# Fourteen pairs of the first feed-forward's up projection by seven products, with all sums of weight blocks made in memory

## The chip, the cores and the metric

The kernel runs on one core of one Trainium2 chip. A core has a matrix engine (TensorE, PE), a vector engine (VectorE, DVE), a scalar engine (ScalarE, ACT), a general engine (GpSimd, POOL) and SyncE (SP), which issues transfers. ACT and POOL can issue transfers too. The metric is device time in microseconds (us) from one launch, lower is better; it is given as the median of several runs, and beside it stands one execution taken by the hardware profiler.

## The reference

What is computed is a trunk of two decoder layers over 512 tokens of 1024 features, in fp32. Cut to what matters:

```python
for i in range(2):
    h = rms_norm(x, pre_g[i])
    h = even_mixer(h, ...) if i == 0 else odd_mixer(h, ...)
    x = x + rms_norm(h, post_g[i])
    h = conv_ffn(rms_norm(x, ffn_pre_g[i]), ffn_w_up[i], ffn_conv_w[i], ffn_conv_b[i], ffn_w_down[i])
    x = x + rms_norm(h, ffn_post_g[i])

def conv_ffn(h, w_up, conv_w, conv_b, w_down):       # w_up: 1024 x 5632, w_down: 2816 x 1024
    u = causal_dwconv(h @ w_up, conv_w, conv_b)      # three taps along the tokens, per feature
    gate, up = split(u, 2)
    return (silu(gate) * up) @ w_down
```

The first mixer runs latent attention (8 heads) and differential attention (4 heads) side by side and projects their joined heads. The second does the same with dilated-window attention (12 heads in three groups) and stick-breaking attention (4 heads).

## The kernel before

**Products.** Every fp32 weight and activation is split into two parts, a rounded one (h) and the rest (l), and a product is three matmuls (`mm3`, L343: h by h, h by l, l by h). The class `Weights` (L43) is the stream of weight tiles: SP loads a tile `wraw` (three buffers), ACT rounds it into `wh` (L81), DVE subtracts to get `wl` (L82), a few tiles ahead of use.

**The two feed-forwards** (`ffn`, L428). The up projection goes over 22 pairs of a gate block and an up block, 128 features each, over 512 tokens. A plain pair is 2 x 8 products of 512 columns (48 matmuls). A pair "by seven products" is the scheme of Strassen and Winograd over a 2 x 2 split: the weight tile of a pair has four blocks (half of the input features by gate or up), the activations have four (half of the features by half of the tokens), and seven block products, of 4 x 3 matmuls of 256 columns each, take the place of eight (84 matmuls). It needs sums of weight blocks and sums of activation blocks (`x_sums`, L488, once for a feed-forward), and puts the results together in PSUM. One half of the results comes out negated for some taps, which `minus` (L435) turns in the convolution's weights.

`SEVEN` (L37) says which pairs go so. In the first feed-forward these are 4, 6, ..., 18, every second one, eight in all. Their weight sums are made on the spot: `up_sums` (L175) loads the pair's two tiles, makes four block sums with DVE (L191, L192, L195, L198) and splits the result, and `seven_sums` (L568) runs the products. In the second feed-forward these are 4 to 17, fourteen in one row, in an order written out by hand (`begin_seven`, `seven`, L610 to L664: the scaling and convolution of one pair stand between the products of the next). Their block sums come ready from memory, as tiles of 128 x 512 next to the plain blocks (`up_blocks`, L204).

**The sums in memory.** `make_sums` (L145) writes them with transfers on POOL's queue. A chunk is three pairs, 384 rows of 512 numbers; four tensors `ws` hold four kinds of sums. A chunk takes eight moves in a chain: plain ones copy a block into `ws`, adding ones add a block to what lies there.

```python
steps = [(0, 3, ALU.bypass), (2, 2, ALU.bypass), (0, 2, ALU.add), (2, 0, ALU.add), (1, None, ALU.bypass),
         (1, 0, ALU.add), (3, -1, ALU.bypass), (3, 1, ALU.add)]
```

Fourteen pairs are five chunks, the last of two pairs. Two chunks (`EARLY`, L40) are moved in the first mixer, after the latent attention's shared norms (call at L1133); three in the second, after its first value products (L1550). A mark goes ahead: a transfer of one number into each first target, from a tile that is written at the place where the moves are to begin, so that they don't start earlier. The order runs chunks against each other with a lag of four steps.

**POOL's other work.** POOL takes its instructions in order. It computes every inverse root of a mean square (`rstd`, L256: L260, L262, L263). In the differential attention it does so for each of 16 units (L1321, L1322): `value` sums squares on ACT, POOL adds epsilon and raises to the power -1/2, and one iteration later `norm` (L1329) multiplies with it on DVE. That stage's loop (L1404) runs in an order written by hand on PE, DVE, ACT and POOL; PE's gaps are filled with projections (`fill`). At the end of the first feed-forward four rows of 128 tokens are normed twice, transposed (L293) and go into the second mixer's value products, in a written order as well. The second mixer's output rows use `rstd` again (L1856, L1862).

Outside the written orders a planner places the instructions of an engine.

Of the kernel before, what the change touches and what calls it, by code (L numbers as in the profile page):

```python
# [9 lines left out]
F32 = mybir.dt.float32  # L10
# [26 lines left out]
SEVEN = range(4, 19, 2), range(4, 18)  # L37
CHUNK = 3
PAIRS = len(SEVEN[1])
EARLY = 2  # L40
# [55 lines left out]
def trunk(tc, A, out):  # L96
# [3 lines left out]
    with ExitStack() as top:  # L100
# [44 lines left out]
        def make_sums(chunks, mark):  # L145

            wide = "(a q) c -> a (q c)"
            if not sums_of:
                sums_of[1] = [[dpool.tile([CHUNK * P, S], F32, tag=f"ws{j}{c}", name="ws")
                               for c in range(-(-PAIRS // CHUNK))] for j in range(4)]  # L150
            tiles = sums_of[1]

            def move(c, j, src, op=ALU.bypass):
                n = min(CHUNK, PAIRS - c * CHUNK) * P
                if src is None:
                    src = tiles[0][c][:n]
                elif src < 0:
                    src = tiles[1][c][:n]
                else:
                    src = A["ffn_up_q"][src, c * CHUNK * P:c * CHUNK * P + n]  # L160
                nc.gpsimd.dma_start(tiles[j][c][:n].rearrange(wide, q=4), src.rearrange(wide, q=4), accum_op=op,
                                    max_dma_last_dim=2048)

            steps = [(0, 3, ALU.bypass), (2, 2, ALU.bypass), (0, 2, ALU.add), (2, 0, ALU.add), (1, None, ALU.bypass),
                     (1, 0, ALU.add), (3, -1, ALU.bypass), (3, 1, ALU.add)]
            with tc.manual_schedule(engines={POOL.engine}):
                for c in chunks:
                    for j in (0, 2):
                        nc.gpsimd.dma_start(tiles[j][c][0:1, 0:1], mark)
                for n in range(len(steps) + 4 * len(chunks)):  # L170
                    for j, c in enumerate(chunks):
                        if 0 <= n - 4 * j < len(steps):
                            move(c, *steps[n - 4 * j])

        def up_sums(src):  # L175


            raws = []
            lo, hi = slice(0, S), slice(S, 2 * S)

            def unit(n):
                if n == 0:
                    for z in range(2):
                        raws.append(wpool.tile([P, 1024], F32, tag="wraw", name="wraw", bufs=3))
                        nc.sync.dma_start(raws[z][:], src[z])
                a, b = raws
                h, l = W.pair()
                if n == 0:
                    W.split(h, l, a, 1024)
                elif n == 1:  # L190
                    DVE.tensor_tensor(a[:, lo], a[:, lo], b[:, lo], ALU.add)  # L191
                    DVE.tensor_tensor(b[:, lo], b[:, lo], b[:, hi], ALU.add)  # L192
                    W.split(h, l, b, 1024)
                elif n == 2:
                    DVE.tensor_tensor(b[:, hi], b[:, hi], a[:, lo], ALU.add)  # L195
                    W.split(h, l, b[:, hi], S)
                else:
                    DVE.tensor_tensor(a[:, hi], a[:, hi], b[:, hi], ALU.add)  # L198
                    W.split(h, l, a, 1024)
                return h, l  # L200

            return [lambda n=n: unit(n) for n in range(4)]

        def up_blocks():  # L204

            def block(i, j):
                if j < 4:
                    return A["ffn_up_q"][j, i * P:(i + 1) * P]
                return sums_of[1][j - 4][i // CHUNK][i % CHUNK * P:(i % CHUNK + 1) * P]

            parts = [lambda i=i, j=j: block(i, j)
                     for i, j in ([(0, 0)] + [(i + (j == 0), j) for i in range(PAIRS)
                                              for j in (4, 1, 5, 0, 6, 7, 3)]) if i < PAIRS]
            return [(tuple(parts[n:n + 2]), S * len(parts[n:n + 2])) for n in range(0, len(parts), 2)]

        def ffn_units(layer):
            up = []
            for f in range(NF):
                if f in SEVEN[0] and layer == 0:
                    up += up_sums(A["ffn_w_up"][layer, f])  # L220
                elif f == SEVEN[1][0] and layer:
                    up += up_blocks()
                elif layer == 0 or f not in SEVEN[1]:
                    up += [(A["ffn_w_up"][layer, f, z], 1024) for z in range(2)]
            return (up + [lambda n=n: down[layer](n) for n in range(4 * HF)])
# [202 lines left out]
        def ffn(layer, xnT, pending, final):  # L428
            with ExitStack() as es:
# [138 lines left out]
                def seven_sums(u, p5):  # L568

                    z1, z2 = u[0][:, :256], u[0][:, 256:]  # L570
                    c21, c22 = u[1][:, :256], u[1][:, 256:]
                    def product(o, w, half, x, fresh):
                        for k in range(4):
                            b = slice(half * S + k * P, half * S + (k + 1) * P)
                            xs = [v[:, k] if isinstance(x, list) else v[:, k * 256:(k + 1) * 256] for v in x]
                            mm3(o, w[0][:, b], w[1][:, b], *xs, fresh and k == 0, k == 3, not fresh)

                    wa = W.next()
                    product(c21, wa, 0, x_block(0, 0), True)
                    ACT.copy(z1, c21)  # L580
                    wb = W.next()
                    p = bank("t", "p5")[:, :256]
                    product(p, wb, 0, sums[0], True)
                    ACT.copy(p5, p)
                    wc = W.next()
                    product(c21, wc, 0, sums[1], False)
                    DVE.tensor_tensor(z2, c21, p5, ALU.add)  # L587
                    product(z1, wa, 1, x_block(4, 0), False)
                    wd = W.next()
                    product(c21, wd, 0, sums[2], False)  # L590
                    DVE.tensor_tensor(c22, c21, p5, ALU.add)
                    product(z2, wd, 1, x_block(4, 256), False)
                    product(c21, wb, 1, sums[3], False)

# [84 lines left out]
                for n, f in enumerate(PAIRED):  # L679
# [6 lines left out]
                    if final and n == pairs[0]:  # L686
                        depth, W.depth = W.depth, 0
                        ready, stop = W.pos + 3, W.pos + (7 * PAIRS + 1) // 2 + 2
                        W.ahead(ready)
                        written = tc.manual_schedule(engines={PE.engine, DVE.engine, ACT.engine})  # L690
                        written.__enter__()
                        begin_seven()
                    if final and n in pairs:
                        left = seven(n, left)
                        if n == pairs[-1]:
                            for step in late:
                                step()
# [4 lines left out]
                    u = u4[2 * n:2 * n + 2] if n < 2 else [bank(t, "u") for t in "sa"] if n in pairs else [None] * 2  # L702
                    y = sp.tile([P, 2, S], F32, tag="y", name="y")
                    if n in pairs:
                        seven_sums(u, y[:, 1, :256])
                    scale, conv, silu, rest = left = evict(n, y, u)
                    for z in range(2):
# [6 lines left out]
                        if z == 0 or not final or n != pairs[0] - 1:  # L714
                            scale(z)
                        if not final or n != pairs[0] - 1:
                            conv(z)
                    if not final or n != pairs[0] - 1:
                        silu()
                        for step in rest:  # L720
                            step()
# [199 lines left out]
        def even():  # L921
            with ExitStack() as es:
# [51 lines left out]
                with ExitStack() as e1:  # L974
# [116 lines left out]
                    with ExitStack() as e2:  # L1091
# [41 lines left out]
                        make_sums(range(EARLY), rk[0:1, 0:1])  # L1133
# [265 lines left out]
                units = [(h, i) for h in range(4) for i in ORDER]  # L1399
                scored, turned_, valued = {}, {}, {}  # L1400
                plan = ((6, 2),) + ((2, 2),) * 11 + ((2, 1),) * 4 + ((1, 0), (1, 1), (1, 2), (0, 2))
                depth, W.depth = W.depth, 0
                with tc.manual_schedule(engines={PE.engine, DVE.engine, ACT.engine, POOL.engine}):
                    for n in range(len(units) + 4):  # L1404
# [13 lines left out]
                        if n >= 2 and n - 2 < len(units):  # L1418
                            valued[n - 2] = value(*units[n - 2])(turned_.pop(n - 2))
                        fill(plan[n][1])  # L1420
# [43 lines left out]
        def odd(xnT, pending, order):  # L1464
            xh, xl = xnT
            with ExitStack() as es:
# [414 lines left out]
def layout(inputs):  # L1881
# [50 lines left out]

    q = r["ffn_w_up"][1, SEVEN[1][0]:SEVEN[1][-1] + 1].reshape(PAIRS, 2, P, 2, S)
    r["ffn_up_q"] = q.transpose(1, 3, 0, 2, 4).reshape(4, PAIRS * P, S)
# [47 lines left out]
```

## Time and profile before

| | |
|---|---|
| median of 3 runs | 1134.77 us (1133.51 to 1138.42) |
| profiled execution, first to last instruction | 1130.8 us |
| PE busy | 1118.5 us, 6432 matmuls |
| DVE busy | 898.1 us |
| ACT busy | 624.9 us |
| POOL busy | 96.0 us |
| moved by DMA | 166.82 MB, 29.36 MB of them on POOL's queue |

The profiled execution has no time of its own beside its span; the median lies 4.0 us above the span, which is what surrounds the first and last instruction. A row of a timeline has the start in us, the duration in us, the engine, the line of the kernel, the operation, output and inputs with their shapes, a count if several are merged, and in brackets how long the engine stood before it and what released it. "PEld" are weight loads, "POOLq" and the like are an engine's sequencer. A DMA row on POOL is the issue of the transfer, not the transfer.

### The profile page before, as it was taken

How to read it: one execution, taken by the hardware profiler on the slowest of the kernel's cores; microseconds unless marked ns; L12 is line 12 of the kernel's file. 1: busy time of each engine (PE TensorE's matmuls, PEld its weight loads, DVE VectorE, ACT ScalarE, POOL GpSimd, SP SyncE). 2: the span in 40 equal slices, each digit the busy share in tenths (PEclk: the TensorE clock that was granted, in tenths of full speed). 3: DMA queues.
4: the chain of work that ended last, by engine and by line, in shares of the span. 5: the costliest groups of instructions: out<-in, count | busy, mean ns of one | idle time of the engine just before them, and what ended most of it. 6: DMA issues, size and time to landing. Idle time of an engine off the chain costs nothing.

```text
span 1130.8 us, 17165 instructions
## 1 busy us (share of the span) xinstructions
PE 1118.5 (99%) x6432; PEld 951.1 (84%) x6432; DVE 898.1 (79%) x1526; ACT 624.9 (55%) x1060; POOL 96.0 (8%) x189
## 2 busy tenths in 40 slices
PE   9999999999999999999999999999999999999997
PEld 8876677898998998887888877888999999988886
DVE  6677476489998898898984476576889999989887
ACT  5565466446555555556653455575456666645662
POOL 2211012220000000000031111102000000000002
PEclk9999999999999999999999999999999999999999
DMA  8666731131422333354737878852335556524461
GB/s 296 197 180 137 215 109 57 57 134 57 130 94 79 128 94 121 99 168 151 226 128 227 206 186 202 217 122 85 110 112 182 179 182 196 177 89 148 144 205 75
DMA packets 61426, 166.82 MB, mean 148 GB/s; under 512 B 7841, under 2 KB 8993, under 8 KB 61217
## 3 DMA queue, kind: packets, MB, share of 16 engines
q1 hardware_dynamic: 47712, 132.65, 36.2%
q0 software_dynamic: 11712, 29.36, 11.8%
q10 hardware_dynamic: 1920, 3.74, 1.0%
q8 instruction: 50, 0.82, 0.3%
q14 instruction: 32, 0.25, 0.1%
HBM read 158.35 MB, written 35.68 MB: 172 GB/s over the span
## 4 chain that ended last, share of the span: by engine, by line
PE 88%; DVE 5%; DMA 3%; issue 2%; ACT 1%; POOL 0%; SPq 0%; POOLq 0%; DVEq 0%; ACTq 0%
PE u L345 12%; PE u L347 12%; PE u L346 12%; PE acc L345 4%; PE acc L346 4%; PE acc L347 4%; PE apt L345 3%; PE apt L346 3%; PE apt L347 2%; PE ao L345 2%; PE ao L347 2%; PE ao L346 2%; DVE wl L82 2%; PE sps L1170 2%; DMA wraw<-in_ffn_w_down 1%
## 5 line engine op out<-in xcount | busy, mean ns | idle before, releaser
L81 ACT CAST wh<-wraw 128x1024 fp32r<-128x1024 f32 (+1 forms) x235 | 240.7, 1033 | 158.0 <-PE u L346 51.6
L82 DVE TENSOR_TENSOR wl<-wraw,wh 128x1024 fp32r<-128x1024 f32 (+1 forms) x235 | 280.6, 1201 | 52.5 <-ACT wh L81 51.9
L345 PE MATMUL u<-xh,wh 128*128 128x256 f32 (+1 forms) x680 | 223.5, 329 | 0.0
L346 PE MATMUL u<-xl,wh 128*128 128x256 f32 (+1 forms) x680 | 223.1, 328 | 0.0
L347 PE MATMUL u<-xh,wl 128*128 128x256 f32 (+1 forms) x680 | 222.9, 328 | 0.0
L345 PEld LDWEIGHTS u<-xh,wh 128*128 128x128 f32 x680 | 129.2, 190 | 12.6 <-DVE u L587 1.3
L347 PEld LDWEIGHTS u<-xh,wl 128*128 128x128 f32 x680 | 129.1, 190 | 11.2 <-DVE wl L82 0.3
L346 PEld LDWEIGHTS u<-xl,wh 128*128 128x128 f32 x680 | 129.3, 190 | 11.0
L345 PE MATMUL acc<-wh,gh 128*128 128x512 f32 (+1 forms) x250 | 96.9, 388 | 0.8 <-DVE uu L758 0.8
L346 PE MATMUL acc<-wl,gh 128*128 128x512 f32 (+1 forms) x250 | 96.9, 388 | 0.0
L347 PE MATMUL acc<-wh,gl 128*128 128x512 f32 (+1 forms) x250 | 96.9, 387 | 0.0
L522 ACT ACTIVATE y<-u,cw 128x512 f32<-128x512 f32 x88 | 67.6, 777 | 36.9 <-PE u L347 33.4
L345 PE MATMUL u<-gh,wh 128*128 128x256 f32 x264 | 74.9, 284 | 0.1
L260 POOL TENSOR_TENSOR rv<-ms,epst 128x1 f32<-128x1 f32 x39 | 12.3, 314 | 736.3 <-ACT junk L312 351.2
L347 PE MATMUL u<-gh,wl 128*128 128x256 f32 x264 | 74.7, 283 | 0.0
L346 PE MATMUL u<-gl,wh 128*128 128x256 f32 x264 | 74.7, 283 | 0.0
L526 DVE SCALAR_TENSOR_TENSOR y<-u,cw,y 128x511 f32<-128x511 f32 x88 | 65.0, 743 | 3.5 <-ACT y L522 3.4
L528 DVE SCALAR_TENSOR_TENSOR y<-u,cw,y 128x510 f32<-128x510 f32 x88 | 65.3, 745 | 1.5
L345 PEld LDWEIGHTS acc<-wh,gh 128*128 128x128 f32 x250 | 46.9, 188 | 11.2 <-DVE uu L758 1.4
L347 PEld LDWEIGHTS acc<-wh,gl 128*128 128x128 f32 x250 | 47.0, 188 | 9.7
L346 PEld LDWEIGHTS acc<-wl,gh 128*128 128x128 f32 x250 | 47.0, 188 | 9.4
L345 PEld LDWEIGHTS u<-gh,wh 128*128 128x128 f32 x264 | 50.6, 192 | 1.3 <-ACT u L580 0.5
(371 smaller groups left out, 2420.8 us busy)
## 6 DMA issues: line engine op xcount, KB each, us to landing
wraw<-in_ffn_w_up SPq DMA_DIRECT2D x60, 512.0 KB, 3.7
wraw<-in_ffn_w_down SPq DMA_DIRECT2D x44, 512.0 KB, 3.7
ws<-in_ffn_up_q POOLq DMA_DIRECT2D x24, 768.0 KB, 7.6
wraw<-ws SPq DMA_DIRECT2D x56, 256.0 KB, 2.9
wraw<-in_ffn_up_q SPq DMA_DIRECT2D x42, 256.0 KB, 2.9
ws<-ws POOLq DMA_DIRECT2D x8, 768.0 KB, 6.4
wraw<-in_od_w_dqk SPq DMA_DIRECT2D x12, 512.0 KB, 4.4
wraw<-in_ffn_w_down SPq DMA_DIRECT2D x22, 256.0 KB, 2.8
```

The lines of the kernel that those rows point to most:

```text
L81: self.nc.scalar.copy(h[:, :w], raw[:, :w])
L82: self.nc.vector.tensor_tensor(l[:, :w], raw[:, :w], h[:, :w].bitcast(F32), ALU.subtract)
L260: POOL.tensor_tensor(v[:, :n], ms, epst[:, :n], ALU.add)
L345: PE.matmul(o, lh, rh, start=first, stop=False, skip_group_check=more)
L346: PE.matmul(o, lh, rl, start=False, stop=False, skip_group_check=more)
L347: PE.matmul(o, ll, rh, start=False, stop=last, skip_group_check=more)
L522: ACT.activation(y[:, z], u[z], AF.Identity, bias=c[:, 3:4], scale=c[:, 2:3])
L526: DVE.scalar_tensor_tensor(y[:, z, 1:], u[z][:, :S - 1], c[:, 1:2], y[:, z, 1:], ALU.mult, ALU.add)
L528: DVE.scalar_tensor_tensor(y[:, z, 2:], u[z][:, :S - 2], c[:, 0:1], y[:, z, 2:], ALU.mult, ALU.add)
L1170: PE.matmul(s_ps[:, :w], mq[h][:, i * P:(i + 1) * P], mk[h][:, :w], start=True, stop=True)
```

## The change

`SEVEN` becomes 4 to 17 in the first feed-forward and 4 to 15 in the second: fourteen pairs and twelve. Both run in the written order with sums from memory, so `up_sums`, `seven_sums` and the exceptions for the last layer go. The tables of blocks are one for each layer.

`sum_steps` gives the moves as a list, step by step over all its chunks (first step of every chunk, then the second, and so on), with one mark in front, into the first chunk's first target. The first feed-forward's five chunks are moved in the first mixer: three where two were moved (24 moves), and the other two, 16 moves, one for each iteration of the differential attention's loop, right after `value`. The second feed-forward's four chunks (32 moves) are moved in the second mixer; their mark now reads the low part of the transposed activations of the last 128 tokens, in place of a number copied after the value products.

```diff
-SEVEN = range(4, 19, 2), range(4, 18)
+SEVEN = range(4, 18), range(4, 16)
 CHUNK = 3
-PAIRS = len(SEVEN[1])
-EARLY = 2
+PAIRS = [len(n) for n in SEVEN]
+CHUNKS = [-(-n // CHUNK) for n in PAIRS]
...
-        def make_sums(chunks, mark):
+        def sum_steps(layer, chunks, mark=None):
...
-            with tc.manual_schedule(engines={POOL.engine}):
-                for c in chunks:
-                    for j in (0, 2):
-                        nc.gpsimd.dma_start(tiles[j][c][0:1, 0:1], mark)
-                for n in range(len(steps) + 4 * len(chunks)):
-                    for j, c in enumerate(chunks):
-                        if 0 <= n - 4 * j < len(steps):
-                            move(c, *steps[n - 4 * j])
-
-        def up_sums(src):
...
+            moves = [lambda c=c, step=step: move(c, *step) for step in steps for c in chunks]
+            if mark is not None:
+                moves.insert(0, lambda: nc.gpsimd.dma_start(tiles[0][chunks[0]][0:1, 0:1], mark))
+            return moves
+
+        def make_sums(layer, chunks, mark):
+            with tc.manual_schedule(engines={POOL.engine}):
+                for move in sum_steps(layer, chunks, mark):
+                    move()
...
-                if f in SEVEN[0] and layer == 0:
-                    up += up_sums(A["ffn_w_up"][layer, f])
-                elif f == SEVEN[1][0] and layer:
-                    up += up_blocks()
-                elif layer == 0 or f not in SEVEN[1]:
+                if f == SEVEN[layer][0]:
+                    up += up_blocks(layer)
+                elif f not in SEVEN[layer]:
                     up += [(A["ffn_w_up"][layer, f, z], 1024) for z in range(2)]
...
-                    if final and n == pairs[0]:
+                    if n == pairs[0]:
                         depth, W.depth = W.depth, 0
-                        ready, stop = W.pos + 3, W.pos + (7 * PAIRS + 1) // 2 + 2
+                        ready, stop = W.pos + 3, W.pos + (7 * PAIRS[layer] + 1) // 2 + 2
...
-                    if final and n in pairs:
+                    if n in pairs:
                         left = seven(n, left)
...
-                        make_sums(range(EARLY), rk[0:1, 0:1])
+                        make_sums(0, range(3), rk[0:1, 0:1])
...
                 units = [(h, i) for h in range(4) for i in ORDER]
+                moves = sum_steps(0, range(3, 5))
...
                             valued[n - 2] = value(*units[n - 2])(turned_.pop(n - 2))
+                            if moves:
+                                moves.pop(0)()
...
-                ACT.copy(lead[0:1, 1:2], st[0:1, 0:1])
-                make_sums(range(EARLY, -(-PAIRS // CHUNK)), lead[0:1, 1:2])
+                make_sums(1, range(CHUNKS[1]), xl[0:1, 0, 3 * P:3 * P + 1].bitcast(F32))
```

More of the change, by code (lines that the diff above doesn't have):

```diff
@@ L143, in trunk, with move @@
         sums_of = {}
-        def make_sums(chunks, mark):
+        def sum_steps(layer, chunks, mark=None):
             wide = "(a q) c -> a (q c)"
[L148 to L154, printed above, removed]
+            if layer not in sums_of:
+                sums_of[layer] = [[dpool.tile([CHUNK * P, S], F32, tag=f"ws{layer}{j}{c}", name="ws")
+                                   for c in range(CHUNKS[layer])] for j in range(4)]
+            tiles = sums_of[layer]
+            def move(c, j, src, op):
+                n = min(CHUNK, PAIRS[layer] - c * CHUNK) * P
                 if src is None:
@@ L159, in move @@
                 else:
-                    src = A["ffn_up_q"][src, c * CHUNK * P:c * CHUNK * P + n]
+                    src = A[f"ffn_up_q{layer}"][src, c * CHUNK * P:c * CHUNK * P + n]
                 nc.gpsimd.dma_start(tiles[j][c][:n].rearrange(wide, q=4), src.rearrange(wide, q=4), accum_op=op,
@@ L175, in up_sums @@
-        def up_sums(src):
[L178 to L202, printed above, removed]
@@ L204, in up_blocks @@
-        def up_blocks():
+            moves = [lambda c=c, step=step: move(c, *step) for step in steps for c in chunks]
[3 more added lines that the diff above has]
+        def make_sums(layer, chunks, mark):
+            with tc.manual_schedule(engines={POOL.engine}):
+                for move in sum_steps(layer, chunks, mark):
+                    move()
+        def up_blocks(layer):
@@ L206, in block @@
             def block(i, j):
                 if j < 4:
-                    return A["ffn_up_q"][j, i * P:(i + 1) * P]
-                return sums_of[1][j - 4][i // CHUNK][i % CHUNK * P:(i % CHUNK + 1) * P]
+                    return A[f"ffn_up_q{layer}"][j, i * P:(i + 1) * P]
+                return sums_of[layer][j - 4][i // CHUNK][i % CHUNK * P:(i % CHUNK + 1) * P]
             parts = [lambda i=i, j=j: block(i, j)
-                     for i, j in ([(0, 0)] + [(i + (j == 0), j) for i in range(PAIRS)
-                                              for j in (4, 1, 5, 0, 6, 7, 3)]) if i < PAIRS]
+                     for i, j in ([(0, 0)] + [(i + (j == 0), j) for i in range(PAIRS[layer])
+                                              for j in (4, 1, 5, 0, 6, 7, 3)]) if i < PAIRS[layer]]
@@ L566, in evict @@
                     return scale, conv, silu, [second, third, fourth, fifth] if n % 2 else [first]
[L568 to L593, printed above, removed]
                 def product(o, x, fresh):
@@ L701, in ffn @@
                         continue
-                    u = u4[2 * n:2 * n + 2] if n < 2 else [bank(t, "u") for t in "sa"] if n in pairs else [None] * 2
+                    u = u4[2 * n:2 * n + 2] if n < 2 else [None] * 2
                     y = sp.tile([P, 2, S], F32, tag="y", name="y")
-                    if n in pairs:
-                        seven_sums(u, y[:, 1, :256])
                     scale, conv, silu, rest = left = evict(n, y, u)
@@ L713, in ffn @@
                                 mm3(u[z], wh[:, b], wl[:, b], xh[:, k], xl[:, k], k == 0, k == KD - 1)
-                        if z == 0 or not final or n != pairs[0] - 1:
+                        if z == 0 or n != pairs[0] - 1:
                             scale(z)
-                        if not final or n != pairs[0] - 1:
+                        if n != pairs[0] - 1:
                             conv(z)
-                    if not final or n != pairs[0] - 1:
+                    if n != pairs[0] - 1:
                         silu()
@@ L1931, in layout @@
     r["ffn_conv"] = cv.reshape(2, 4, 2, NF, P)[:, :, :, PAIRED].transpose(0, 4, 3, 2, 1)
-    q = r["ffn_w_up"][1, SEVEN[1][0]:SEVEN[1][-1] + 1].reshape(PAIRS, 2, P, 2, S)
-    r["ffn_up_q"] = q.transpose(1, 3, 0, 2, 4).reshape(4, PAIRS * P, S)
+    for n, pairs in enumerate(SEVEN):
+        q = r["ffn_w_up"][n, pairs[0]:pairs[-1] + 1].reshape(len(pairs), 2, P, 2, S)
+        r[f"ffn_up_q{n}"] = q.transpose(1, 3, 0, 2, 4).reshape(4, len(pairs) * P, S)
     r["ev_pre_gb"] = np.broadcast_to(a["ev_pre_g"], (P, D))
```

## The prediction

> **What bounds the kernel now.** I read the page first (busy shares, the slices with the granted clock, the chain by engine), then the stretches of the two up projections, then the timelines of POOL, DVE and ACT around the places where the change puts its transfers.
>
> ```profile
> span 1130.8 us, 17165 instructions
> PE 1118.5 (99%) x6432; PEld 951.1 (84%) x6432; DVE 898.1 (79%) x1526; ACT 624.9 (55%) x1060; POOL 96.0 (8%) x189
> PEclk9999999999999999999999999999999999999999
> PE 88%; DVE 5%; DMA 3%; issue 2%; ACT 1%; POOL 0%; SPq 0%; POOLq 0%; DVEq 0%; ACTq 0%
> ```
>
> TensorE is busy 99% of the span at the full granted clock, in every slice, and carries 88% of the chain that ended last. So a matmul that goes is time won, and any wait that reaches PE is time lost: nothing else is slack. POOL has 8% of work, and the chain does not touch it. The median of the three runs, 1134.77 us, stands 4.0 above this span; I take those 4.0 us as unchanged and count from 1134.8.
>
> **Step 1, the matmuls.** In the first FFN 8 of 22 pairs go by seven products before and 14 after; in the second 14 before and 12 after. Stretches of the two up projections (window, PE busy, matmul records, clock, DMA share, GB/s), and scale steps on ACT (L522), one per half pair:
>
> ```profile
> 235.50:474.00 238.50, 238.31 (x1458) 1.00 0.34 108
> 787.10:1019.00 231.90, 231.75 (x1674) 1.00 0.48 152
> ```
> ```profile
> 844.77 0.77 ACT L522 ACTIVATE y<-u,cw 128x512 f32<-128x512 f32 x1
> ...
> 965.36 0.78 ACT L522 ACTIVATE y<-u,cw 128x512 f32<-128x512 f32 x1 [1.56 <-PE u L347]
> ...
> 1009.01 0.78 ACT L522 ACTIVATE y<-u,cw 128x512 f32<-128x512 f32 x1
> ...
> 1019.89 0.78 ACT L522 ACTIVATE y<-u,cw 128x512 f32<-128x512 f32 x1
> ```
>
> Twelve pairs by seven products lie between the first two rows: 120.6 / 12 = 10.05 us each. One plain pair lies between the last two: 10.88 us. A pair is thus worth 0.83 us, not the eighth of 10.88 (1.36) that the count of products suggests. The second up projection, with 14 pairs, the written order and sums from memory, takes 231.9 us; the first gets the same make, so 238.5 becomes 231.9: -6.6. The second loses two pairs: +1.7. Sum -4.9 us.
>
> The first FFN also loses the sums made on DVE (four additions for each of the 8 pairs) and their splits change shape; SP gets 56 more, smaller loads there. I cost both at nothing: PE's busy time fills both stretches but for 0.2 us, so DVE's relief was hidden already, and the second FFN runs the same loads with no more idle time. If the loads came late, PE would wait at a pair's first product; nothing in the second stretch shows that.
>
> **Step 2, the sums beside the first mixer.** Here the change moves work into POOL's in-order stream. Before, 4 marks and 16 moves (two chunks) stand ahead of the differential attention; after, 1 mark and 24 moves (three chunks), and 16 more go one by one between that stage's POOL steps (L1321, L1322). POOL's timeline of before:
>
> ```profile
> 36.62 2.32 POOL L169 DMA_DIRECT2D ws<-rr  x4 [0.33 <-POOL rr L263]
> 40.64 1.23 POOL L161 DMA_DIRECT2D ws<-in_ffn_up_q  x2 [1.70 <-DMA ws<-rr]
> 48.10 1.02 POOL L161 DMA_DIRECT2D ws<-in_ffn_up_q  x1 [6.24 <-issue]
> 57.42 0.97 POOL L161 DMA_DIRECT2D ws<-in_ffn_up_q  x1 [8.30 <-issue]
> 64.63 0.63 POOL L161 DMA_DIRECT2D ws<-ws  x1 [6.24 <-issue]
> 65.25 0.64 POOL L161 DMA_DIRECT2D ws<-in_ffn_up_q  x1
> 75.97 0.99 POOL L161 DMA_DIRECT2D ws<-in_ffn_up_q  x1 [10.08 <-issue]
> 82.98 0.62 POOL L161 DMA_DIRECT2D ws<-in_ffn_up_q  x1 [6.02 <-issue]
> ...
> 89.68 0.99 POOL L161 DMA_DIRECT2D ws<-in_ffn_up_q  x1 [5.49 <-issue]
> ...
> 137.12 0.95 POOL L161 DMA_DIRECT2D ws<-in_ffn_up_q  x1 [6.11 <-DMA ws<-ws]
> 137.73 0.45 POOL L1260 MEMSET epsp<- 128x1 f32 x1
> 141.53 0.19 POOL L1321 TENSOR_TENSOR st<-st,epsp 128x1 f32<-128x1 f32 x1 [3.35 <-issue]
> 141.79 0.56 POOL L1322 TENSOR_TENSOR rr<-st,mhalf 128x1 f32<-128x1 f32 x1
> ```
>
> The reader is to see the gaps. Two plain moves go out together, or one adding move (the issues of about 1 us), and then POOL stands 5 to 10 us before the next. The idle time is mostly put down to "issue", that is, to nothing recorded. At 82.98 a plain move into another chunk waits behind the adding move of 75.97, though its source is an input and its target was free. So the wait belongs to the queue, not to the data, and interleaving more chunks doesn't remove it. Before, the 16 moves make 13 such groups, 12 steps from 40.64 to 137.12: 8.04 us each, the usual step being about 7.2 (75.97 to 82.98 is 7.0, 82.98 to 89.68 is 6.7, 57.42 to 64.63 is 7.2).
>
> After, the order is step by step over three chunks: 6 plain, 6 adding, 3 plain, 3 adding, 3 plain, 3 adding. In groups that is 3+6+2+3+2+3 = 19, so 18 steps, starting at about 39.0 (40.64 less three of the four marks, 2.32 / 4 each). At 7.2 the last move goes out at 39 + 130 = 169; at the mean of 8.04, at 184. Whether three plain moves may go together no row shows; if so there are 16 groups, 15 steps, 108 us and some 8 for the longer plain groups: 155. I take 169, since most steps are near 7.2.
>
> What is queued behind them: the memset and the first L1321/L1322 pair. These need about 2 us after the last issue (0.6 + 0.45 + 0.27 + 0.55). Who waits for it:
>
> ```profile
> 144.99 0.35 DVE L1329 SCALAR_TENSOR_TENSOR otok<-otok,rr,subg 128x128 f32<-128x128 f32 x1
> 149.69 0.35 DVE L1329 SCALAR_TENSOR_TENSOR otok<-otok,rr,subg 128x128 f32<-128x128 f32 x1
> ```
>
> DVE runs a written order there, and the norm of L1329 stands in it ahead of the next combination and scores. With POOL at 171, the first norm moves from 144.99 to 171: 26 us. PE can go on with one iteration's fill products and then needs DVE's scores, and it has no idle time later to give back. The second L1321 stands behind the first of the interleaved moves, which waits for the last adding move: free at 169 + 7.2 = 176.2, its norm at 178 instead of 149.69 + 26 = 175.7, 2 us more. The other interleaved moves come one per iteration (4.7 us by the two rows); an adding step takes 7.2, a plain one half of that, so over a pair they keep pace, with a result one iteration early as reserve. Step 2: +28 us. Bounds: 155 gives 12 + 2 = 14; 184 gives 41 + 2 = 43.
>
> ```profile
> ws<-in_ffn_up_q POOLq DMA_DIRECT2D x24, 768.0 KB, 7.6
> ```
>
> By the Trainium skill, DMA: Bandwidth & Descriptors, the section on the anatomy of one DMA on the gpsimd path, such a transfer takes about 2.0 us plus its bytes at 436 GB/s, an estimate of 3.8 us for 768 KB. The plain pair of 40.64 agrees (7.46 for two), the adding move of 57.42 (7.21) does not; by the page's figure POOL would be free at about 126 and step 2 would cost nothing, which is the first rival's result. By the same skill, TensorE: Matmul & The Clock Gate, Part 1, a PE left idle for about 3.4 us falls to half its clock until it has worked as long; the clock row above has no such place before, and a stop of 26 us would add an estimated 2 us, which the sum leaves out.
>
> **Step 3, the sums beside the second mixer.** The mark now reads the transposed activations, not a copy made at the end of the value products, so the built order puts 8 plain moves among the last POOL steps of the first FFN, and all four chunks (32 moves) ahead of the second mixer's output norms. Timelines of POOL, DVE and PE in before:
>
> ```profile
> 594.47 0.55 POOL L263 TENSOR_TENSOR rr<-rv,mhalf 128x1 f32<-128x1 f32 x1
> ...
> 613.52 1.28 POOL L161 DMA_DIRECT2D ws<-in_ffn_up_q  x2 [0.90 <-DMA ws<-lead]
> 626.34 1.01 POOL L161 DMA_DIRECT2D ws<-in_ffn_up_q  x1 [11.55 <-issue]
> ...
> 747.35 0.88 POOL L161 DMA_DIRECT2D ws<-in_ffn_up_q  x1 [3.53 <-DMA ws<-ws]
> 767.93 0.19 POOL L260 TENSOR_TENSOR rv<-ms,epst 128x1 f32<-128x1 f32 x1 [19.70 <-ACT junk L312]
> ```
> ```profile
> 595.05 1.41 DVE L878 SCALAR_TENSOR_TENSOR t<-X,rr,gain 128x512 f32<-128x512 f32 x2 [1.15 <-POOL rr L263]
> ```
> ```profile
> 597.90 1.04 PE L293 MATMUL tp<-ident,t 128*128 128x128 f32 x8
> ```
>
> In the tail the moves start about 583. If four plain ones may stand in the queue, the last L263 (594.47) comes some 3 us late; if two, some 10. The slack from it to PE's transpose is 597.90 - 596.46 = 1.4, so PE waits 1.5 to 9 us. I take 3, nearer the end at which plain moves overlap, because here they are the cheap kind. Ahead of the output norms there were 18 groups in 133.8 us (613.52 to 747.35), 7.87 a step; after, 24 groups, 23 steps, 181 us from 584: 765, by the ends 7.2 and 9 a step 750 and 791. L260 is due at 767.93, or a little later by the tail's own delay. That costs 0 to 20; I take 2, since the mean just meets the due time. Step 3: +5 (1.5 to 12 together, as a late tail also moves the due time).
>
> **Sum.** -4.9 + 28 + 5 = +28: 1163 us.
>
> **Rivals.**
> First, no wait in POOL, so only step 1: 1134.8 - 4.9 = 1130, the other side. Its mechanism is that moves of three chunks overlap where those of two did not: at 3.7 us a move, the pace of the pair at 40.64, 23 steps end at 124. It decides if the last of the 24 moves is issued by 142. For it speaks that after a step each chunk's predecessor is long done; against it the move of 82.98, which had no predecessor and waited. Chance 0.12.
> Second, the wait is longer than forecast in both mixers: 184 and 791 above, +43 and +20, which gives 1193. For it speak the slow steps (48.10 to 57.42 is 9.3, 64.63 to 75.97 is 11.3, and the first of the second mixer 12.8); against it stand the more frequent ones near 7. Chance 0.08.
> Forecast with step 2 between 14 and 43 and step 3 between 1.5 and 12: 1145 to 1185, chance 0.80.
>
> **Numbers.** The predicted time is the forecast's, the range its bounds; what is left out is the two rivals, 0.20. Half a per cent, 5.7 us, is about the smallest change that a measurement of this kernel can tell from no change. The first rival stands at -0.4%, so its 0.12 is split: 0.05 faster, 0.07 within. All else is slower: 0.88.
>
> **What would show it.** In the changed kernel POOL's last unbroken move before L1321's successor lies at 155 to 184 and PE has a hole of over 10 us just after its start in the differential attention; the first up projection takes 232 us and the second 234. The prediction is wrong if the first of the POOL steps still runs at about 142, or if DVE's norm is late while PE is not.

## The result and the profile after

The changed kernel takes 1182.53 us (median; 1182.12 to 1188.4) against 1134.14 for the kernel before in the same comparison: a ratio of 1.042, with a 95% interval of 1.039 to 1.046. The profiled execution spans 1180.3 us, against 1130.8.

These lines of the changed kernel's page stand against the first fence of the prediction (busy times, granted clock by slices of 29.5 us, chain by engine):

```profile
PE 1122.2 (95%) x6576; PEld 959.9 (81%) x6576; DVE 888.1 (75%) x1504; ACT 629.8 (53%) x1069; POOL 118.2 (10%) x213
PEclk9999959989999999999999999999999999999999
PE 74%; issue 16%; POOL 4%; DMA 3%; DVE 1%; ACT 1%; SPq 0%; POOLq 0%; DVEq 0%; ACTq 0%
```

PE has about the same work (the count of matmuls rises by 144, many of them shorter), but a smaller share of the span; the sixth slice of the clock row has 5 where there was 9, and "issue" and POOL now hold 20% of the chain that ended last. POOL's timeline around the start of the differential attention (the same places are L1262 and L1263 here, L1321 and L1322 before):

```profile
166.04 0.97 POOL L161 DMA_DIRECT2D ws<-in_ffn_up_q  x1 [6.80 <-issue]
173.20 0.95 POOL L161 DMA_DIRECT2D ws<-in_ffn_up_q  x1 [6.18 <-issue]
173.79 0.47 POOL L1201 MEMSET epsp<- 128x1 f32 x1
174.34 0.18 POOL L1262 TENSOR_TENSOR st<-st,epsp 128x1 f32<-128x1 f32 x1
174.60 0.56 POOL L1263 TENSOR_TENSOR rr<-st,mhalf 128x1 f32<-128x1 f32 x1
...
196.58 1.02 POOL L161 DMA_DIRECT2D ws<-in_ffn_up_q  x1 [4.83 <-issue]
...
204.34 0.95 POOL L161 DMA_DIRECT2D ws<-in_ffn_up_q  x1 [5.88 <-issue]
...
212.34 1.01 POOL L161 DMA_DIRECT2D ws<-in_ffn_up_q  x1 [6.19 <-issue]
...
219.26 0.93 POOL L161 DMA_DIRECT2D ws<-in_ffn_up_q  x1 [5.05 <-issue]
```

The last of the 24 moves is issued at 173.20; the memset and the first root stand right behind it. Then four adding moves, each in an iteration of its own, stand 7 to 8 us apart. What DVE and PE make of it, in their timelines (L1270 is L1329 before):

```profile
175.20 0.35 DVE L1270 SCALAR_TENSOR_TENSOR otok<-otok,rr,subg 128x128 f32<-128x128 f32 x1 [30.36 <-POOL rr L1263]
...
182.71 0.35 DVE L1270 SCALAR_TENSOR_TENSOR otok<-otok,rr,subg 128x128 f32<-128x128 f32 x1 [4.09 <-POOL rr L1263]
...
206.18 0.35 DVE L1270 SCALAR_TENSOR_TENSOR otok<-otok,rr,subg 128x128 f32<-128x128 f32 x1 [2.23 <-POOL rr L1263]
...
214.24 0.35 DVE L1270 SCALAR_TENSOR_TENSOR otok<-otok,rr,subg 128x128 f32<-128x128 f32 x1 [3.04 <-POOL rr L1263]
...
221.08 0.35 DVE L1270 SCALAR_TENSOR_TENSOR otok<-otok,rr,subg 128x128 f32<-128x128 f32 x1 [5.22 <-POOL rr L1263]
```
```profile
148.26 0.40 PE L317 MATMUL aqk<-xh,wl 128*128 128x512 f32 x1
176.41 0.45 PE L906 MATMUL tpp<-ident,s 128*128 128x128 f32 x1 [27.76 <-DVE s L1245]
...
177.37 0.77 PE L315 MATMUL aqk<-xh,wh 128*128 128x512 f32 x1
...
179.65 0.51 PE L317 MATMUL aqk<-xh,wl 128*128 128x512 f32 x1
```

The first norm waits 30 us for POOL, and PE stands for 27.76 us from 148.7 on. Behind the hole a matmul of 512 columns takes 0.63 to 0.77 us until 179.65, where 0.40 was usual ahead of it. By stretches (length, busy times of PE, its weight loads, DVE, ACT and POOL, then granted clock, DMA share, GB/s):

```profile
145.00:173.00 28.00, 3.66 (x15) 1.83 (x13) 0.00 (x0) 1.36 (x4) 3.78 (x5) 0.64 0.71 173
173.00:178.00 5.00, 1.59 (x7) 1.52 (x8) 2.73 (x9) 1.09 (x3) 1.80 (x4) 0.50 0.64 94
178.00:200.00 22.00, 20.26 (x101) 14.27 (x100) 13.49 (x39) 13.47 (x41) 8.71 (x15) 0.96 0.74 213
200.00:225.00 25.00, 20.16 (x103) 13.42 (x101) 11.89 (x38) 11.62 (x36) 6.66 (x12) 1.00 0.82 171
225.00:250.00 25.00, 20.24 (x101) 15.71 (x99) 8.95 (x31) 10.73 (x37) 9.34 (x18) 0.93 0.67 170
250.00:281.00 31.00, 30.11 (x136) 24.90 (x137) 17.09 (x23) 12.90 (x28) 8.38 (x18) 0.94 0.39 94
281.20:513.10 231.90, 231.68 (x1672) 219.67 (x1671) 211.41 (x286) 137.43 (x183) 2.32 (x5) 1.00 0.52 159
834.90:1068.20 233.30, 233.16 (x1601) 217.49 (x1600) 206.35 (x278) 132.46 (x177) 2.75 (x7) 1.00 0.46 144
```

From 200 to 250 PE stands for about a fifth of the time, in pieces of some us, and the two last rows are the up projections, 231.9 and 233.3 us. The ledger, by the starts of the first and last matmul of each stage in the traces:

| stage, ends at (before / after) | before | after | difference |
|---|---|---|---|
| start to first up projection (235.5 / 281.2) | 235.5 | 281.2 | +45.7 |
| first up (473.6 / 513.1) | 238.1 | 231.9 | -6.2 |
| first down, norms, first value products (605.4 / 652.7) | 131.8 | 139.6 | +7.8 |
| rest of second mixer (786.8 / 834.7) | 181.4 | 182.0 | +0.6 |
| second FFN to the last product (1123.9 / 1173.3) | 337.1 | 338.6 | +1.5 |

The sum is +49.4 us, and the spans differ by 49.5.

### The profile page after: what moved, and what is told of

It reads as the page before. It is cut to its first block, busy times and chain, and to the rows that moved or that the text cites. A ratio compares the mean times of both kernels' runs of the same rounds, so it can differ in the third digit from the quotient of the medians.

```text
span 1180.3 us, 17608 instructions
## 1 busy us (share of the span) xinstructions
PE 1122.2 (95%) x6576; PEld 959.9 (81%) x6576; DVE 888.1 (75%) x1504; ACT 629.8 (53%) x1069; POOL 118.2 (10%) x213
## 4 chain that ended last, share of the span: by engine, by line
PE 74%; issue 16%; POOL 4%; DMA 3%; DVE 1%; ACT 1%; SPq 0%; POOLq 0%; DVEq 0%; ACTq 0%
PE u L315 12%; PE u L317 12%; PE u L316 12%; PE acc L315 6%; PE acc L316 6%; PE acc L317 6%; PE apt L315 2%; PE apt L316 2%; PE apt L317 2%; POOL ws L161 2%; PE ao L317 1%; PE ao L315 1%; PE ao L316 1%; DMA ws<-ws 1%; PE p L317 1%
## 5 line engine op out<-in xcount | busy, mean ns | idle before, releaser
L81 ACT CAST wh<-wraw 128x1024 fp32r<-128x1024 f32 x237 | 245.1, 1047 | 155.7 <-PE u L316 50.0
L82 DVE TENSOR_TENSOR wl<-wraw,wh 128x1024 fp32r<-128x1024 f32 x237 | 287.0, 1219 | 51.4 <-ACT wh L81 50.8
L315 PE MATMUL u<-xh,wh 128*128 128x256 f32 (+1 forms) x664 | 212.0, 319 | 0.0
L316 PE MATMUL u<-xl,wh 128*128 128x256 f32 (+1 forms) x664 | 211.8, 319 | 0.0
L317 PE MATMUL u<-gh,wl 128*128 128x256 f32 x312 | 88.3, 283 | 0.0
L315 PE MATMUL u<-gh,wh 128*128 128x256 f32 x312 | 88.3, 283 | 0.0
L316 PE MATMUL u<-gl,wh 128*128 128x256 f32 x312 | 88.3, 283 | 0.0
L161 POOL DMA_DIRECT2D ws<-in_ffn_up_q x54 | 46.5, 861 | 282.0 <-issue 271.8
L316 PEld LDWEIGHTS u<-gl,wh 128*128 128x128 f32 x312 | 59.9, 192 | 0.1
L317 PEld LDWEIGHTS u<-gh,wl 128*128 128x128 f32 x312 | 59.9, 192 | 0.0
```

The lines of the kernel that those rows point to most:

```text
L81: self.nc.scalar.copy(h[:, :w], raw[:, :w])
L82: self.nc.vector.tensor_tensor(l[:, :w], raw[:, :w], h[:, :w].bitcast(F32), ALU.subtract)
L315: PE.matmul(o, lh, rh, start=first, stop=False, skip_group_check=more)
L316: PE.matmul(o, lh, rl, start=False, stop=False, skip_group_check=more)
L317: PE.matmul(o, ll, rh, start=False, stop=last, skip_group_check=more)
```

## The experiments

The theory: POOL's compute steps wait behind moves that queue ahead of them, and PE waits for those steps. The rivals: the moves slow other things by their traffic, or the new make of the feed-forwards costs something by itself.

**No moves.** The sums' tiles are read from plain blocks of the same size.

```diff
-return sums_of[layer][j - 4][i // CHUNK][i % CHUNK * P:(i % CHUNK + 1) * P]
+return A[f"ffn_up_q{layer}"][j - 4, i * P:(i + 1) * P]
...
-make_sums(0, range(3), rk[0:1, 0:1])
-moves = sum_steps(0, range(3, 5))
+moves = []
-make_sums(1, range(CHUNKS[1]), xl[0:1, 0, 3 * P:3 * P + 1].bitcast(F32))
```

> The changed kernel without any of the moves in memory: the blocks of sums are read from the plain blocks instead, so the outputs are not the reference's, while every product, load into SBUF and split stays. Theory (the whole loss comes from POOL's steps waiting behind the moves): only the gain in matmuls is left, 1134.1 - 4.9 = 1129 us. Rival (the longer row of pairs by seven products costs time itself in the first feed-forward, by late loads or by DVE's order): above 1140.

Measured: 1124.88 us, ratio 0.991 (0.988 to 0.994) to before, span 1123.2. So the whole loss is the moves' doing: with them the span is 57.1 us longer, and the rival, that the new make costs something by itself, fell. The gain without them is larger than forecast; this kernel also lacks the 40 moves that the kernel before makes. By the same ledger: start -1.4, first up -6.2, first down and norms -1.5, second FFN +1.6. The -1.5 is in the first down projection and what follows it: in the kernel before PE waits there for DVE, and here that group is gone, which accounts for 1.0 of the 1.5.

```profile
PE acc L345 <- DVE uu L758: 1.0, 2, 0.8
```

**Moves of the first mixer alone, then of the second alone.**

```diff
 def block(i, j):
+    if layer:          # second kernel: if not layer
+        return A[f"ffn_up_q{layer}"][j - 4, i * P:(i + 1) * P]
...
-make_sums(1, range(CHUNKS[1]), xl[0:1, 0, 3 * P:3 * P + 1].bitcast(F32))     # second kernel: the first mixer's instead
```

> As the run without moves, but the first feed-forward's 40 moves are made as in the change (24 in one row, 16 in the loop); the second feed-forward's blocks of sums are the plain ones. Theory: 1129 plus what the first mixer lost between the two traces (45.7 us), 1175 us. Rival (the moves cost by the memory traffic they add, which is in proportion to their number, 40 of 72, of 53 us): 1158.

> The other half: only the second feed-forward's 32 moves are made, the first's blocks of sums are the plain ones. Theory: 1129 plus the 8 us that the tail of the first feed-forward and the second mixer lost, 1137 us. Rival (traffic, 32 of 72 moves of 53 us): 1153.

Measured: 1172.82 (span 1171.0) and 1136.36 (span 1134.6), one execution each, both near the theory's figures and far from the rival's. Against no moves that is 47.8 and 11.4 us of span; together 59.2, where both at once cost 57.1. PE's waits in the second of the two kernels:

```profile
PE tp L265 <- DVE t L821: 4.5, 2, 2.5
PE av L319 <- DVE xl L226: 2.4, 1, 2.4
```

Both lie in the tail of the first feed-forward, which takes 9.6 us more than without moves; the stage of the output norms, behind the last move, takes 1.4 more.

**Only the 24 moves in a row.**

```diff
 def block(i, j):
+    if layer or i >= 9:
+        return A[f"ffn_up_q{layer}"][j - 4, i * P:(i + 1) * P]
-moves = sum_steps(0, range(3, 5))
+moves = []
-make_sums(1, range(CHUNKS[1]), xl[0:1, 0, 3 * P:3 * P + 1].bitcast(F32))
```

> Only the 24 moves ahead of the differential attention; no interleaved ones and none in the second mixer (plain blocks in their place). Theory: 1129 plus the hole of PE (28 us) and a few us at half clock after it, 1160 us, so that the 16 interleaved moves carry the other 15 of the first mixer's loss. Rival (as I had predicted, interleaved moves keep pace and cost 2): 1172.

Measured: 1155.87, span 1154.1, in one execution. The first up projection starts at 264.4, where it was 234.1 without moves and 282.1 with all of the first mixer's: the row of 24 costs 30.3 us, and the 16 interleaved ones, by difference, 17.7.

**Roots off POOL, moves kept.** A sum and a reciprocal on DVE take the place of POOL's two steps from the differential attention to the second mixer, at the place of use (the root itself is left out), and the 16 interleaved moves follow the 24 on POOL behind a mark of their own.

```diff
-POOL.tensor_tensor(st[:, 7:8], st[:, 7:8], epsp[:], ALU.add)
-POOL.tensor_tensor(r[:], st[:, 7:8], mhalf[:, 0:1], ALU.pow)
-return r
+def make():
+    DVE.tensor_tensor(st[:, 7:8], st[:, 7:8], epsp[:], ALU.add)
+    DVE.reciprocal(r[:], st[:, 7:8])
+    return r
+return Later(make)
...
-moves = sum_steps(0, range(3, 5))
+moves = sum_steps(0, range(3, 5), epsp[0:1, 0:1])
```

> All 72 moves stay, and the seven products too. But from the first mixer's moves to the end of the second mixer no inverse root is made on POOL: DVE adds epsilon and takes a reciprocal in its place, right before the instruction that uses it. The root is left out (a reciprocal stands for it), so the outputs are not the reference's. The 16 moves of the differential attention follow the 24 at once, behind a mark. Theory (POOL's order is the cause): the wait is gone while the traffic is the same, 1129 to 1134 us. Rival (traffic of the moves): about 1182 as before.

Measured: 1159.39 us, ratio 1.022 (1.019 to 1.025): a miss. PE's longest wait and POOL's timeline in this kernel tell why:

```profile
PE tpp L928 <- DVE s L1268: 30.6, 3, 29.9
```
```profile
174.67 0.95 POOL L161 DMA_DIRECT2D ws<-in_ffn_up_q  x1 [6.06 <-issue]
175.26 0.47 POOL L1224 MEMSET epsp<- 128x1 f32 x1
```

One POOL step was left in the path: the memset of the number that DVE's sum reads still stands behind the 24 moves, and the hole stays as it was. Behind the hole nearly all is as without moves, though: the first up starts 34.0 us later than there, 3.7 more than with the row of 24 alone, the tail takes what it takes there (130.3 us), and the rest is some 2 us longer. So the next kernel moves that one instruction.

```diff
-POOL.memset(epsp[:], P * EPS)
+DVE.memset(epsp[:], P * EPS)
```

> The changed kernel with all of its 72 moves, and no step of POOL left in the path of the first mixer: the roots are a sum and a reciprocal on DVE as in the run before this one (the root is left out, so the output is another), and the number that DVE's sum reads, epsp, is now written by DVE too, where it stood behind the 24 moves on POOL. Theory (the time goes to POOL steps that stand behind moves, not to the traffic): PE's wait for the turn of about 30 us goes, the first up projection starts at 234 to 240 against 268, and the time is 1125 to 1132, near the kernel without moves (1124.9). Rival (the traffic of 24 moves itself slows the loads of the first mixer): the hole stays in part, 1140 to 1160.

Measured: 1133.57 us (1130.2 to 1139.03), ratio 1.000 (0.998 to 1.002), 1.6 us above the theory's range and below the rival's. The hole is gone; the one memset was worth 25.8 us. The issue of the 24th move is at 175.65 here, hardly later than in the changed kernel (173.20), and nobody waits for it. So of the 57.7 us between no moves and the changed kernel, 49.0 vanish when no POOL step of the path stands behind the moves. That the other 8.7 are the traffic's is argued, not shown: DVE also has more to do here. In the profiled execution, at 1137.9 one of the longer ones, the span is 12.9 us above that without moves: 8.0 before the first up projection and 5.0 in it. The waits in these two places:

```profile
DVE s L917 <- DMA mmask<-in_mla_mask: 4.3, 1, 4.3
mmask<-in_mla_mask ACTq DMA_DIRECT2D x1, 256.0 KB, 7.7
ACT wh L81 <- DMA wraw<-in_ffn_w_up: 5.8, 2, 4.3
PE tp L285 <- DVE t L1308: 3.2, 1, 3.2
```
```profile
mmask<-in_mla_mask ACTq DMA_DIRECT2D x1, 256.0 KB, 2.9
```

The last line is the changed kernel's. A mask of 256 KB, loaded just in time on ACT's queue, took 7.7 us from issue to landing, and PE stood 3.5 us for it; ACT waited for weights of the up projection shortly before PE stood 3.2 us for DVE. But the mask's 2.9 us in the changed kernel, and 2.7 with the row of 24 alone, were measured with the same moves under way (2.7 without any). In those two kernels the mask's packets ran ahead of an adding move's, here behind them. So the late mask is no part of the changed kernel's loss; whether moves delay such a load depends on which comes first by about a microsecond.

**Smaller moves.** One pair in place of three, so 72 early moves, three in each iteration, 96 in the second mixer: the same bytes. If POOL's queue limits the bytes that are under way, small adding moves can overlap; if each has to land before the next may start, they cannot.

```diff
-CHUNK = 3
+CHUNK = 1
-make_sums(0, range(3), rk[0:1, 0:1])
+make_sums(0, range(9), rk[0:1, 0:1])
-moves = sum_steps(0, range(3, 5))
+moves = sum_steps(0, range(9, 14))
-if moves:
-    moves.pop(0)()
+for _ in range(3):
+    if moves:
+        moves.pop(0)()
```

> The change with chunks of one pair instead of three: the same bytes in three times as many moves of a third of the size (72 ahead of the differential attention, 40 in its loop, up to three an iteration, 96 in the second mixer), all in POOL's order as in the change. [...] Rival (each adding move has to land before the next one may start, whatever its size): 36 adding moves of at least 3.5 us make it later than in the change, above 1200 us.

Measured: 1141.07 us, ratio 1.006 (1.004 to 1.007). POOL's timeline:

```profile
132.04 0.82 POOL L161 DMA_DIRECT2D ws<-in_ffn_up_q  x1 [5.54 <-issue]
...
143.37 0.83 POOL L161 DMA_DIRECT2D ws<-in_ffn_up_q  x1 [0.79 <-issue]
145.59 0.82 POOL L161 DMA_DIRECT2D ws<-in_ffn_up_q  x1 [1.39 <-issue]
146.92 0.81 POOL L161 DMA_DIRECT2D ws<-in_ffn_up_q  x1 [0.51 <-issue]
147.45 0.40 POOL L1201 MEMSET epsp<- 128x1 f32 x1
```

Seven steps lie between the first and the last move shown (four moves between them are left out), 2.13 us each; three of them take 6.4 us, where one adding move of 768 KB mostly takes 7 to 8. The row ends at 146.92 instead of 173.20, so the rival fell, and PE's longest wait ahead of a transpose (`tpp`) is 3.6 us instead of 27.8:

```profile
PE tpp L906 <- DVE s L1245: 3.6, 1, 3.6
```

A POOL step behind such a move waits some 2 us, not 8. Against no moves the profiled execution still loses 10.9 us before the first up projection and 4.7 in the tail.

**Moves where POOL is idle.** The moves are of one pair again. Since POOL does nothing in the first up projection, 48 of its 112 small moves go there (64 stay early), and the second mixer's mark is put back to where it was before. A second kernel puts the second feed-forward's 96 moves there, too.

```diff
+if layer == 0:                                   # in ffn, behind its first products
+    make_sums(0, range(8, 14), xl[0:1, 0, 0:1].bitcast(F32))
+    make_sums(1, range(CHUNKS[1]), xl[0:1, 0, 0:1].bitcast(F32))      # second kernel only
...
-make_sums(1, range(CHUNKS[1]), xl[0:1, 0, 3 * P:3 * P + 1].bitcast(F32))
+ACT.copy(lead[0:1, 1:2], st[0:1, 0:1])                                # first kernel only
+make_sums(1, range(CHUNKS[1]), lead[0:1, 1:2])
```

> Moves of one pair in place of three. First FFN: 64 moves (8 pairs) in a row in the first mixer, none between the steps of the differential attention, the other 48 (6 pairs) behind the first FFN's first products, where POOL has no other work for over 300 us. Second FFN: 96 moves behind a number copied after the value products of the second mixer, as in the kernel before. Theory (POOL's steps wait only for moves that are issued ahead of them): the last early move goes out at about 136, the first of the differential attention's steps on POOL at about 141, the first up projection starts at 234 to 238, the tail of the first FFN takes what it takes without moves, and the time is 1126 to 1131, below the kernel before. Rival (moves of one pair cost by their traffic and number, wherever they stand): 1137 to 1141, as the kernel with moves of one pair in the old places.

> As the run before, but the second FFN's 96 moves also go behind the first FFN's first products, so that 144 moves lie beside its up projection and none beside the second mixer. Theory: POOL stands idle there until about 560, 144 moves at 1.5 us are 216 us and end at about 460, so nothing waits: 1125 to 1130. Rival (the moves share the DMA engines with the loads of the weights, whose share is 0.34 to 0.48 there, and PE waits for weights): the first up projection takes over 240 us against 232, and the time is 1135 or more.

Measured: 1144.75 (ratio 1.009, 1.007 to 1.012) and 1168.46 (ratio 1.030, 1.028 to 1.032). Both times are above the theory's: the second is its rival's, and the first lies even nearly 4 us above its rival's range. In the first kernel the early moves end at 133.68, and no POOL step of the first mixer waits for one, as the theory said; all the same the profiled span is 19.9 us above that without moves: 7.4 before the first up projection (the mask, 8.0 us to land, stops PE for 3.8), 8.2 in it, none in the tail and 4.1 in the second mixer. Stretches of the first up projection and the waits between 300 and 480 us, in the second kernel:

```profile
300.00:330.00 30.00, 27.27 (x223) 26.59 (x222) 23.36 (x32) 16.24 (x23) 11.56 (x17) 1.00 1.06 300
330.00:360.00 30.00, 21.22 (x172) 20.46 (x170) 19.95 (x27) 14.23 (x20) 14.39 (x27) 0.98 1.03 360
```
```profile
ACT wh L81 <- DMA wraw<-ws: 44.6, 24, 3.8
ACT wh L81 <- DMA wraw<-in_ffn_up_q: 28.2, 17, 3.6
PE u L315 <- DVE u L588: 19.1, 10, 5.4
```

The DMA engines are full (share 1.03 to 1.06, against 0.52 over this projection in the changed kernel), the weights land late, and the delay goes by ACT and DVE to PE. This up projection takes 263.2 us, with 48 moves 240.1, without moves 231.9. Beside a stage that streams weights the traffic itself is the cost.

## Why the prediction was right in kind, and 20 us short

The forecast was 1163 us with a range of 1145 to 1185; the time is 1182.5, so the direction, the mechanism and its place came out, and the sum was 49 where 28 was said. That the time still lies inside the range is partly luck: step 2 alone passed its upper bound (43 us said at most, 45.7 by the ledger), and step 3 made up for it with 8.4 of the 12 us that it was allowed.

- Step 1 said -4.9. Without moves the gain is 7.6 us of span. The up projections do what was said (231.9 and 233.3, for 231.9 and 233.6). The term for DVE's relief, put at nothing, was wrong by up to 1.5: the up projection hides it, the down projection behind it does not. Another 1.4 comes from the first mixer, where two chunks' moves of before are gone, too (PE's one wait of 1.2 us ahead of a transpose, `tpp`, goes with them); the changed kernel does not have this part.
- Step 2, the row of 24: last issue at 169 said, 173.20 measured; first norm at 171 said, 175.20 measured. The groups were somewhat misjudged (after the first two, plain moves go out singly, some 3 us apart, and the adding steps are mostly a little longer than 7.2, two of them over 10), and the errors cancelled in part. Measured alone, the row costs 30.3 us, for 26 said. The plain pair's 7.46 us were read as two transfers of 3.7; in the trace the two overlap and land 5.5 and 6.5 us after their issues.
- Step 2, the interleaved moves: here the sum failed. It said that "over a pair they keep pace" and charged 2 us. By difference they cost 17.7. The averaging over a pair was the mistake: the order goes step by step over two chunks, so after four plain moves come four adding ones, in four iterations of 4.7 us that each take 7 to 8 (196.58 to 219.26 above). The reserve of one iteration is used up at the first of them; after that about 3 us an iteration reach PE.
- The half clock was left out with an estimate of 2 us. The rows show somewhat more: from 176.41 to 179.65, 3.2 us, at half speed, some 1.6 us lost, and the two stretches at 0.93 and 0.94 behind hold one piece of 3.4 us at half speed each, which takes up to 1.7 more each time. The Trainium skill, TensorE: Matmul & The Clock Gate, Part 1, says that full speed comes back after about 3.4 us of work, and the trace's 3.2 us agree with that.
- Step 3, the tail: 3 us said, 7.8 measured, and 9.3 against the kernel without moves. One L263 was thought late; POOL's timeline has five single moves, each ahead of another step of the roots, so a wait of mostly 3 us is paid for several rows of tokens:

```profile
628.27 0.59 POOL L161 DMA_DIRECT2D ws<-in_ffn_up_q  x1 [3.03 <-issue]
628.87 0.58 POOL L233 TENSOR_TENSOR rr<-rv,mhalf 128x1 f32<-128x1 f32 x1
...
634.45 0.59 POOL L161 DMA_DIRECT2D ws<-in_ffn_up_q  x1 [2.92 <-issue]
635.06 0.58 POOL L233 TENSOR_TENSOR rr<-rv,mhalf 128x1 f32<-128x1 f32 x1
```

- Step 3, the output norms: 2 us said, 0.6 measured. The last move goes out at 816.80 and the due step follows at 817.43, as "the mean just meets the due time" had it, with all of it shifted by the 47 us that were lost up to there.
- The first rival (moves of three chunks overlap, 1130) fell: the steps keep 7 to 8 us. The second (longer waits, 1193) had the total nearer, but by another sum: neither the row nor the output norms were at their upper ends.
- The 4.0 us between span and median were no constant: an execution's time lies 1.7 to 3.4 us above its own span in the runs here (1182.12 for a span of 1180.3), and the rest was spread between executions. So the spans differ by 49.5 us, the medians by 48.4.

When a move is let in, the landings in the traces show. In the changed kernel POOL stood for over 1 us ahead of 61 moves; all but two, which wait for their marks, start 0.26 to 0.36 us after an earlier move landed (the adding moves of 71.96, 79.35 and 86.39 after landings at 71.65, 79.03 and 86.08). The move that they build on had landed long before (for 71.96 at 48.98), so it is the queue, as step 2 read it, and not the data. All 36 adding moves start with no other move under way, plain ones with at most one. Of the moves of 256 KB most adding ones start with two others under way, and plain ones with up to six. That is why three small adding moves overlap where a large one stands alone. What sets this limit isn't shown; a larger queue was not tried. Whether the 8.7 us can be avoided (an earlier mask, say) stays open, too. No kernel here that makes all the sums was faster than the kernel before: by the medians the kernel without moves gains 9 to 10 us, and that is about what the moves still cost where no POOL step waits.

## What to carry to other kernels

A transfer that stands in an engine's in-order stream is also a wait of every compute step behind it, however little that engine is busy; so look for the first step behind the row and for who needs it, down to a memset. Interleaving pays only if each single step, not their mean, is shorter than the period it is put into; here many small transfers did better than few large ones (1141.07 us against 1182.53). Before moving transfers to an idle engine's time, read the DMA share of that stretch and add what the transfers will bring: with 1.03 to 1.06 the weights that come just in time were late here.

## What the runs showed of the hardware that was not expected

Adding moves of 768 KB stand mostly 7 to 8 us apart on POOL's queue, because each waits until no other move is under way; those of 256 KB, up to three of which are under way together, 2.13 us on the mean in the row shown. So the bytes go only a little faster (6.4 us for the same 768 KB), but a POOL step behind a move waits much less. An unrelated load of 256 KB on another queue landed 2.6 to 2.9 us after its issue in the four kernels where its packets started ahead of an adding move's of 768 KB, and after 7.7 us where they started behind it (first packet at 65.30, the move's from 61.69 to 68.27). By the Trainium skill, DMA: Bandwidth & Descriptors, Queues, rings and completion order, each DMA engine serves its queues in turn, packet by packet; this agrees with the two queues' packets running side by side from 65.30 to 68.27, but not with 4.0 us from the issue to the first packet, which no run here explains.
